# Output weights loaded seven chunks ahead, and background sums pinned in issue order and marked on both halves

## The chip, the cores and the metric

The kernel runs on one core of one Trainium2 chip. The metric is the device time of one execution in microseconds (us). The engines are TensorE (PE in the profile, with PEld for its weight loads), VectorE (DVE), ScalarE (ACT), GpSimd (POOL) and SyncE (SP), which here only issues DMAs. Sixteen DMA engines move the data: q1 is the queue that SP's transfers use, q0 the one that GpSimd's use.

## The reference

One decoder layer on 512 tokens of width 2048, in float32. The input is normalised and multiplied by one wide matrix; its columns are split into the latents of an MLA branch (8 heads, decoupled rotary key), the queries, keys and values of a forgetting-attention branch ("fox", 8 heads), and a gate for each. Both branches run causal softmax attention, are gated, joined and multiplied by `w_out`; the result is normalised and added to the input.

```python
h = _rms_norm(x, g_pre)
proj = h @ w_in
(q_lat, kv_lat, k_rope_raw, gate_mla, fq, fk, fv, f_logit, gate_fox) = jnp.split(proj, split_points, axis=-1)
o_mla = _mla_branch(q_lat, kv_lat, k_rope_raw, ...) * jax.nn.silu(gate_mla)
o_fox = _fox_branch(fq, fk, fv, f_logit, b_forget) * jax.nn.silu(gate_fox)
o = jnp.concatenate([o_mla, o_fox], axis=-1) @ w_out
return x + _rms_norm(o, g_post)
```

## The kernel before

**Precision.** A float32 operand is used as a sum of two reduced-precision parts, hi and lo. A product is three matmuls, hi by hi, hi by lo and lo by hi (`mm3`, lines 150 to 152).

**Weights.** They come in chunks of up to 128 x 1024, numbered in the order of use in one list (220 chunks). `load` issues the DMA of chunk i into a tile raw (lines 242 and 259 issue it on SP). `divide` makes whi by a cast on ACT (line 279) and wlo by a subtraction on DVE (line 282). `chunk(i, ahead_load=4, ahead=2)` is called where chunk i is needed: it loads up to chunk i + ahead_load and divides up to i + ahead. The whi and wlo tiles are three deep. Where a raw tile lies is decided in `raw_tile` (line 224): six buffers of a pool of its own in the stage of the latents and MLA gates (`deep`), a slot, a pool of three buffers called wp, or, late in the output stage, every other three chunks a second pool of three (`more`). Slots are 28 places of 4 KB a partition (line 88) that hold most other tiles: normalised input, head operands, gates, fetched operands, partial results.

**Fewer products.** The blocked products (values v, latents l, MLA gates m, the values of the MLA branch u, and the output, o) are done with seven half-size products in place of eight, named p1, p2, p4, q6, g7, g5 and g3. Some need sums of weight blocks, t7, t6, t5 and t4. Sums of activations are made on DVE, and most are put away in HBM by GpSimd (`away_steps`, line 944; its stores are line 953, tiles awaymg and awayog) and fetched again by SP (line 987).

**Sums of weights.** Some are made when the chunk is used: the second block is loaded beside the first (line 250) and joined on DVE (line 269); joins are asked for up to two chunks before the division. The rest are made in the background, in HBM, by DMAs alone. The list `bg` holds, in order, the tiles of v, l, m, u and o. `add_step(n)` (line 314) does three things: GpSimd accumulates the second block into tile n-1 (line 320), SP copies the first block into tile n (line 324), and SP copies 16 numbers of the weight tile just used into tile n+1 (line 326), a mark: the next step's copy writes the same bytes, so it has to wait for the mark, and the mark for that weight tile. So a step is tied to the progress of the products. For u a block is a strided view with four dimensions and is moved in two halves of 512 columns (`alike`, line 306); the mark lies in the first.

**When steps come.** `paced` (line 561) counts finished pieces of products and calls `add_step` when the pace is reached; tiles of o are twice as wide and count double. The pace is 20, 8, 12 and 4.9 in turn, 1000 (none) from line 1429 to line 1505, and 4.5 after it.

**Order.** A scheduler arranges each engine's instructions at compile time from its own estimate of when each is ready; the order of the source gives the priority. `in_order` (line 132) pins an instruction behind what was traced before it on its engine; the joins are pinned so, and the casts while `deep` is set.

**Stages in time.** First projection, to about 42 us; values and fox gates, to about 230; fox heads, to about 425; the products of latents and MLA gates, to about 580; MLA heads, to about 730; then the output products (lines 1755 to 1825), which hold 56 chunks. `three` (line 1789) issues six of the fourteen output products. Each product takes its chunks by the loop in `product` (line 1030).

Of the kernel before, what the change touches and what calls it, by code (L numbers as in the profile page):

```python
# [16 lines left out]
ALU = mybir.AluOpType  # L17
# [49 lines left out]
def tile_hybrid_layer(  # L67
# [16 lines left out]
    nc = tc.nc  # L84
    pe, act, dve, pool = nc.tensor, nc.scalar, nc.vector, nc.gpsimd
# [14 lines left out]
    def slot(name, dt=F32, shape=(P, 2, S)):  # L100

        return sp.tile(list(shape), dt, tag="s", name=name)
# [29 lines left out]
    def in_order(*instructions):  # L132

        for i in instructions:
            tc.keep_in_program_order(i)
# [13 lines left out]
    def mm3(o, ah, al, bh, bl, first, last, **kw):  # L149
        pe.matmul(o, ah, bh, start=first, stop=False, **kw)  # L150
        pe.matmul(o, ah, bl, start=False, stop=False, **kw)  # L151
        pe.matmul(o, al, bh, start=False, stop=last, **kw)  # L152
# [55 lines left out]
    def add_chunks(w, cols, nk, per, width, first_k=0, single=0):  # L208


        first = len(chunks)
        k = 0
        while k < nk:
            n = min(1 if k < single else per, nk - k)
            chunks.append((w, cols, first_k + k, n, width))
            k += n
        return range(first, len(chunks))

    raws, ready, up_chunks, early = {}, {}, set(), set()
# [4 lines left out]
    def raw_tile(i):  # L224
        if deep and deep[1] <= i < deep[2] and (i - deep[1]) % (DEEP + 3) < DEEP:
            return deep[0].tile([P, 1024], F32, tag="raw", name=f"raw{i}", bufs=DEEP)
        if i in up_chunks:
            return slot(f"raw{i}", shape=(P, 1024))
        if i <= prods["g7", "v"][-1] and i % 5 < 2:
            return vr.tile([P, 1024], F32, tag="raw", name=f"raw{i}", bufs=2)  # L230
        pool = more[0] if more and (i - more[1]) % 6 < 3 else wp
        return pool.tile([P, 1024], F32, tag="raw", name=f"raw{i}", bufs=3)

    def load(i, small=None):

        w, cols, k, n, width = chunks[i]
        assert state["step"] >= needs.get(i, -3) + 2
        if cols is None:

            raw = raw_tile(i)  # L240
            for a, b in alike(raw, w):
                nc.sync.dma_start(a, b)
            raws[i] = raw
            if k is not None:
                if seconds and i not in early:
                    pool, bufs = seconds
                    second = pool.tile([P, 2, 512], F32, tag="second", name=f"second{i}", bufs=bufs)
                else:
                    second = slot(f"second{i}")
                nc.sync.dma_start(second, k)  # L250
                raws[i] = raw, second.rearrange("p k c -> p (k c)")
            return
        if i < 2:
            raw = slot(f"raw{i}", shape=(P, 1024))
        else:
            raw = raw_tile(i)
        v = raw[:, : n * width].rearrange("p (k c) -> p k c", k=n)
        for at, off, cnt in cols:
            (nc.sync if cnt >= P or small is None else small).dma_start(
                v[:, :, at : at + cnt],  # L260
                w[0, k * P : (k + n) * P, off : off + cnt].rearrange("(k p) c -> p k c", p=P),
            )
        raws[i] = raw

    def join(i):

        if isinstance(raws.get(i), tuple):
            raw, second = raws[i]
            tc.keep_in_program_order(dve.tensor_tensor(out=raw, in0=raw, in1=second, op=ALU.add))  # L269
            raws[i] = raw  # L270
# [16 lines left out]
    def prepare(i):  # L287
        while state["divided"] < min(len(chunks), i + 1):
            divide(state["divided"])
            state["divided"] += 1  # L290

    def chunk(i, ahead_load=4, ahead=2):
        upto = i + ahead_load
        if deep:
            upto = max(upto, min(i + DEEP + 2, deep[2] - 1, state["loaded"] + i % 2))
        while state["loaded"] < min(len(chunks), upto + 1):
            load(state["loaded"])
            state["loaded"] += 1
        prepare(i + ahead)
        for k in range(i + ahead + 1, min(state["loaded"], i + ahead + (3 if deep else 2))):  # L300
            join(k)
        return ready.pop(i)

    W, made = {}, {}
    bg = []

    def alike(to, w):

        if len(w.shape) == 4:
            to = to.rearrange("p (k h x) -> p k h x", k=2, h=4)  # L310
            return [(to[:, k], w[:, k]) for k in range(2)]
        return [(to if len(w.shape) == 2 else to.rearrange("p (k c) -> p k c", k=2), w)]

    def add_step(n, mark):


        if n > 0:
            to, _, second = bg[n - 1]
            for a, b in alike(to, second):
                pool.dma_start(a, b, accum_op=ALU.add)  # L320
        if 0 <= n < len(bg):
            to, first, _ = bg[n]
            for a, b in alike(to, first):
                nc.sync.dma_start(a, b)
        if n + 1 < len(bg):
            nc.sync.dma_start(bg[n + 1][0][0:1, 0:16], mark)

    def sum_blocks(g, block, late, width=512, nj=4):

# [14 lines left out]
    prods = {}  # L344
# [43 lines left out]
    first = add_chunks(w_in, [(0, O_KR - L4, KL), (KL, O_F, NH)], NK, 2, KL + NH, single=2)  # L388
# [157 lines left out]
    def pump(n=1):  # L546
        for _ in range(n):
            if todo:
                todo.popleft()()
# [11 lines left out]
    def paced(w):  # L561

        if state["step"] <= len(bg):
            state["tiles"] += 1
            wide = 0 <= state["step"] < len(bg) and bg[state["step"]][0].shape[1] > 1024
            pace = state["pace"] * (1 + wide)
            if state["tiles"] >= pace:
                state["tiles"] -= pace
                add_step(state["step"], w[0:1, 0, 0:16].bitcast(F32))
                state["step"] += 1  # L570
# [367 lines left out]
    def head_steps(j, names, raw_of, place):  # L938

        return operand_steps("o", j, (o_of[K1[j]], o_of[K2[j]]), names, raw_of, place)  # L940
# [53 lines left out]
    def divisions(n, of):  # L994
        return [lambda j=j: part_fetched(n, of, j) for j in range(2 if of == "o" else 4)]
# [13 lines left out]
    def product(name, g, parts, o, first, last, rate=1, at=None, held=0, side=(), turned=False):  # L1009


        side = deque(side)
        kk = 0

        def step(j, kk, t, hi, lo):
            if not turned:
                mm3(
                    o[t], *parts(kk, t), hi[:, j, :], lo[:, j, :], first and kk == 0, last and kk == 7,
                    skip_group_check=True,
                )  # L1020
                return
            for f in range(2):
                c = slice((2 * t + f) * P, (2 * t + f + 1) * P)
                mm3(
                    o[t][:, f * HALF : (f + 1) * HALF], hi[:, j, c], lo[:, j, c], *parts(kk),
                    first and kk == 0 and f == 0, last and kk == 7, skip_group_check=True,
                )

        rng = list(prods[name, g])
        for i in rng[: len(rng) - held]:  # L1030
            hi, lo = chunk(i)
            for j in range(2):
                if at is not None and kk == at[0]:
                    at[1]()
                for t in range(2):
                    step(j, kk, t, hi, lo)
                kk += 1
                pump(rate)
                paced(hi)
                if side and not held and kk % 2 == 0:  # L1040
                    side.popleft()()
        w = [chunk(i, ahead=0) for i in rng[len(rng) - held :]]
        if w:
            side.popleft()()
        for t in range(2):
            for m in range(2 * len(w)):
                step(m % 2, kk + m, t, *w[m // 2])
            if w:
                finish(t, 2, o[t])
# [172 lines left out]
    todo.extend([*fs[13:], *rot[:3]])  # L1222
    A = two_of(proj_bank, "va")
    product("p1", "v", x_block(0, 0), A, True, True)
    drain()
    pa, pb = v_block("vpa"), v_block("vpb")
# [306 lines left out]
    def halves(a):  # L1533
        return [a[:, t, :] for t in range(2)]
# [55 lines left out]
    for p in range(4):  # L1590
        if p == 3:
            first = divisions("a11", "o") + [s for j in (2, 3) for s in head_steps(j, ("a11",), tmp, part_slot)]
# [3 lines left out]
        if p == 0:  # L1596
# [3 lines left out]
            p1 = slot("up1")  # L1600
            for t in range(2):
                act.copy(p1[:, t, :], A[t])
            p1 = halves(p1)
# [150 lines left out]
    p1 = [slot(f"p1{g}") for g in range(2)]  # L1754
# [6 lines left out]
    p1 = [halves(a) for a in p1]  # L1761
# [99 lines left out]
```

## Time and profile before

| | us |
|---|---|
| median of 3 runs | 895.2 (894.72 to 896.06) |
| the profiled execution | 896.48 |
| its span, first to last instruction | 894.7 |
| mean granted TensorE clock | 0.995 |
| moved by DMA | 225.07 MB, mean 252 GB/s |

The profile is of one execution. A line of the timeline is start, duration, engine (a q behind it: its sequencer), source line, operation, what it writes and reads (buffer numbers left out), count, and in brackets the idle time before it and what ended that. In the list of waits a line is who waited, for whom, the total, how often and the longest. A line of the chain of waits is start, duration and what the chain ran through.

### The profile page before, as it was taken

To read this page: it belongs to the slowest core of one execution; us is meant where nothing else is said; L and a number is where in the kernel's file an instruction comes from. 1 tells how busy PE (TensorE), PEld (TensorE's weight loads), DVE (VectorE), ACT (ScalarE), POOL (GpSimd) and SP (SyncE) were. 2 spreads that over 40 slices of the span, in tenths; PEclk is the share of its full clock that TensorE was granted. 3 is DMA by queue.
4 is the path that set the end of the run, shared out by engine and by line. 5 is a ranking of instruction groups with operands and counts; after the bars stand their busy time and mean duration, and the time that the engine had idled before them with its cause. 6 is when DMAs were issued, how large, how long until landed. Compare 5 with 4: busy or idle time off the path is not lost.

```text
span 894.7 us, 12701 instructions
## 1 busy us (share of the span) xinstructions
PE 882.5 (99%) x4486; PEld 748.8 (84%) x4486; DVE 660.3 (74%) x1106; ACT 462.5 (52%) x841; POOL 72.9 (8%) x92
## 2 busy tenths in 40 slices
PE   9999999999999999999999999999999999999996
PEld 9988887888888888888998999787888888888885
DVE  4679995548656636476588898978787895988785
ACT  7944443334344424345545565546465776646383
POOL 0111110001111211010000000000000000000021
PEclk9999999999999999999999999999999999999998
DMA  9998798889899998897899884799878537799878
GB/s 304 298 269 237 204 358 275 247 224 316 260 280 271 249 229 210 234 254 178 270 411 407 322 294 141 152 278 201 209 166 215 151 113 236 226 326 320 265 211 249
DMA packets 139235, 225.07 MB, mean 252 GB/s; under 512 B 16898, under 2 KB 68892, under 8 KB 138148
## 3 DMA queue, kind: packets, MB, share of 16 engines
q1 hardware_dynamic: 124660, 184.19, 63.3%
q0 software_dynamic: 13776, 39.85, 21.8%
q8 instruction: 35, 0.57, 0.2%
q10 hardware_dynamic: 736, 0.22, 0.1%
q14 instruction: 28, 0.23, 0.1%
HBM read 209.53 MB, written 69.22 MB: 312 GB/s over the span
## 4 chain that ended last, share of the span: by engine, by line
PE 87%; DMA 6%; DVE 3%; ACT 2%; issue 1%; SPq 0%; POOL 0%; ACTq 0%; DVEq 0%; POOLq 0%
PE fq L150 3%; PE fk L150 3%; PE fk L152 3%; PE fk L151 3%; PE fq L152 3%; PE fq L151 3%; PE in L614 3%; PE sm L657 3%; PE fg L150 2%; PE fg L151 2%; PE fg L152 2%; PE oa L150 2%; PE oa L152 2%; PE oa L151 2%; PE sf L657 2%; DMA raw<-t4u 1%
## 5 line engine op out<-in xcount | busy, mean ns | idle before, releaser
L282 DVE TENSOR_TENSOR wlo<-raw,whi 128x1024 fp32r<-128x1024 f32 (+3 forms) x220 | 260.7, 1188 | 135.7 <-ACT whi L279 128.8
L279 ACT CAST whi<-raw 128x1024 fp32r<-128x1024 f32 (+3 forms) x220 | 224.3, 1023 | 233.5 <-PE fk L151 35.3
L150 PE MATMUL fk<-h,whi 128*128 128x512 f32 x128 | 52.5, 410 | 0.0
L150 PE MATMUL fq<-h,whi 128*128 128x512 f32 x128 | 50.8, 397 | 0.0
L150 PE MATMUL fg<-h,whi 128*128 128x512 f32 x128 | 50.3, 393 | 0.0
L152 PE MATMUL fk<-h,wlo 128*128 128x512 f32 x128 | 50.2, 392 | 0.0
L151 PE MATMUL fk<-h,whi 128*128 128x512 f32 x128 | 50.1, 392 | 0.0
L152 PE MATMUL fq<-h,wlo 128*128 128x512 f32 x128 | 50.0, 390 | 0.0
L151 PE MATMUL fq<-h,whi 128*128 128x512 f32 x128 | 49.9, 390 | 0.0
L152 PE MATMUL fg<-h,wlo 128*128 128x512 f32 x128 | 49.9, 390 | 0.0
L151 PE MATMUL fg<-h,whi 128*128 128x512 f32 x128 | 49.8, 389 | 0.0
L675 ACT ACTIVATE pf<-pf,stf 128x128 f32<-128x128 f32 (+3 forms) x32 | 18.0, 562 | 61.1 <-DVE stf L666 61.1
L269 DVE TENSOR_TENSOR raw<-raw,second 128x1024 f32<-128x1024 f32 x32 | 39.0, 1218 | 0.4 <-DMA second<-in_w_out_dram 0.4
L614 PE MATMUL in<-whi,h 128*128 128x328 f32 x128 | 30.0, 321 | 0.0
L150 PE MATMUL mq<-ln,whi 128*128 128x512 f32 x72 | 29.2, 406 | 0.0
L152 PEld LDWEIGHTS fk<-h,wlo 128*128 128x128 f32 x128 | 24.0, 188 | 5.5
L152 PEld LDWEIGHTS fq<-h,wlo 128*128 128x128 f32 x128 | 24.0, 188 | 5.3
L152 PEld LDWEIGHTS fg<-h,wlo 128*128 128x128 f32 x128 | 24.0, 188 | 5.1
L151 PE MATMUL mq<-ln,whi 128*128 128x512 f32 x72 | 28.2, 392 | 0.0
L152 PE MATMUL mq<-ln,wlo 128*128 128x512 f32 x72 | 28.2, 392 | 0.0
L151 PEld LDWEIGHTS fg<-h,whi 128*128 128x128 f32 x128 | 24.1, 188 | 4.7
L150 PEld LDWEIGHTS fg<-h,whi 128*128 128x128 f32 x128 | 24.0, 188 | 4.7
(610 smaller groups left out, 2418.9 us busy)
## 6 DMA issues: line engine op xcount, KB each, us to landing
raw<-in_w_in_dram SPq DMA_DIRECT2D x96, 512.0 KB
raw<-in_w_out_dram SPq DMA_DIRECT2D x32, 512.0 KB
second<-in_w_in_dram SPq DMA_DIRECT2D x24, 512.0 KB
bmg<-awaymg SPq DMA_DIRECT2D x20, 256.0 KB
awaymg<-rmg POOLq DMA_DIRECT2D x8, 512.0 KB, 7.7
raw<-t6v SPq DMA_DIRECT2D x8, 512.0 KB
t7o<-in_w_out_dram SPq DMA_DIRECT2D x4, 1024.0 KB
t7o<-in_w_out_dram POOLq DMA_DIRECT2D x4, 1024.0 KB, 11.7
```

The costliest lines, as they stand in the source:

```text
L150: pe.matmul(o, ah, bh, start=first, stop=False, **kw)
L151: pe.matmul(o, ah, bl, start=False, stop=False, **kw)
L152: pe.matmul(o, al, bh, start=False, stop=last, **kw)
L269: tc.keep_in_program_order(dve.tensor_tensor(out=raw, in0=raw, in1=second, op=ALU.add))
L279: cast = act.copy(hi[:, :m], raw[:, :m])
L282: dve.tensor_tensor(out=lo[:, :m], in0=raw[:, :m], in1=hi[:, :m].bitcast(F32), op=ALU.subtract)
L614: pe.matmul(banks[t][:, :n], a[k][:, tss[t]], b[:, j, :], start=k == 0 and m == 0, stop=k == NK - 1 and m == 2,)
L657: pe.matmul(s[:, :nn], a[:, qs], c[:, :nn], start=(i == 0), stop=(i == len(pairs) - 1))
L675: act.activation(p, p, AF.Exp, bias=st[:, 0:1], scale=unit, accum_out=st[:, 1:2])
```

## The change

Three edits, in `raw_tile`, `add_step` and `product`.

- In the output products a chunk's call loads up to seven chunks ahead; elsewhere four, as before. From the first output chunk on, each chunk whose number is a multiple of three has its raw tile in a slot.
- GpSimd's accumulation of a background sum is pinned behind what was traced before it on GpSimd.
- Where a background tile is moved in two halves (u, four tiles), each half gets a mark.

```diff
     def raw_tile(i):
         if deep and deep[1] <= i < deep[2] and (i - deep[1]) % (DEEP + 3) < DEEP:
             return deep[0].tile([P, 1024], F32, tag="raw", name=f"raw{i}", bufs=DEEP)
-        if i in up_chunks:
+        if i in up_chunks or i >= prods["p1", 0][0] and i % 3 == 0:
             return slot(f"raw{i}", shape=(P, 1024))
...
         if n > 0:
             to, _, second = bg[n - 1]
             for a, b in alike(to, second):
-                pool.dma_start(a, b, accum_op=ALU.add)
+                in_order(pool.dma_start(a, b, accum_op=ALU.add))
         if 0 <= n < len(bg):
             to, first, _ = bg[n]
             for a, b in alike(to, first):
                 nc.sync.dma_start(a, b)
         if n + 1 < len(bg):
-            nc.sync.dma_start(bg[n + 1][0][0:1, 0:16], mark)
+            to, first, _ = bg[n + 1]
+            nc.sync.dma_start(to[0:1, 0:16], mark)
+            if len(first.shape) == 4:
+                nc.sync.dma_start(to[0:1, 512:528], mark)
...
         for i in rng[: len(rng) - held]:
-            hi, lo = chunk(i)
+            hi, lo = chunk(i, 7 if g in (0, 1) else 4)
```

## The prediction

> **What bounds the kernel now.** I read the page first, then the list of TensorE's waits.
>
> ```profile
> span 894.7 us, 12701 instructions
> ...
> PE 882.5 (99%) x4486; PEld 748.8 (84%) x4486; DVE 660.3 (74%) x1106; ACT 462.5 (52%) x841; POOL 72.9 (8%) x92
> ```
> ```profile
> PE mix L1706 <- ACT scaler L1705: 2.2, 1, 2.2
> PE sm L657 <- ACT mw L127: 1.1, 1, 1.1
> PE warm L169 <- DVE warm L164: 1.1, 1, 1.1
> PE vg L151 <- DVE wlo L282: 0.7, 1, 0.7
> PE gcm L151 <- DVE wlo L282: 0.6, 1, 0.6
> PE uC L150 <- DVE mk L140: 0.5, 1, 0.5
> PE od L151 <- DVE wlo L282: 0.3, 1, 0.3
> ```
>
> TensorE is busy in 882.5 of 894.7 us, so an edit gains only what it takes out of the few waits, and costs whatever new wait it makes. In the list a row is who waited, for whom, us in total, times, longest. The waits that better fed weights could shorten are those for wlo: 0.7, 0.6 and 0.3, together 1.6 us. Only the last, at tile od, lies in the output stage, where the deeper loading acts. The others (mix, sm, warm, uC) end on arithmetic of ACT and DVE that no edit touches.
>
> So the three edits are searched for new waits. Two touch queues outside the output stage, and the one that looks like bookkeeping, the pinning of GpSimd's accumulating DMAs, moves the most. I went on to the timeline of POOL's instructions.
>
> ```profile
> 189.88 1.17 POOL L320 DMA_DIRECT2D t7l<-in_w_in_dram  x1 [3.02 <-DMA t7l<-in_w_in_dram]
> 210.55 1.50 POOL L1194 DMA_DIRECT2D v_away<-vc  x2 [19.50 <-DVE vc L1152]
> ...
> 394.65 0.81 POOL L320 DMA_DIRECT2D t4o<-t6o  x1 [11.88 <-DMA t6o<-t7o]
> ...
> 406.03 1.16 POOL L320 DMA_DIRECT2D t7o<-in_w_out_dram  x1 [9.80 <-DMA t7o<-in_w_out_dram]
> ...
> 459.89 0.53 POOL L953 DMA_DIRECT2D awayog<-rog  x1 [1.81 <-DVE rog L963]
> 567.29 0.88 POOL L320 DMA_DIRECT2D t6o<-t7o  x1 [106.86 <-DMA t6o<-in_w_out_dram]
> ```
> ```profile
> 558.49 0.26 SPq L326 DMA_DIRECT2D t6o<-whi  x1
> ```
>
> These rows run out of the source's order. One background step issues, in this order, the accumulation of tile n-1 (line 320), the first load of tile n (324) and the mark of tile n+1 (326). The mark of the second t6o came at 558.49, because the pace is 1000 between lines 1429 and 1505. The same step accumulates the first t4o, and that ran at 394.65; the next step's accumulation, of the second t7o, ran at 406.03. The scheduler hoisted both by some 160 us, ahead of the awayog stores, which the source issues from line 1444 on, inside the products of lines 1452 and 1458.
>
> **The change part by part.** *Pinning line 320.* A pinned instruction comes after everything traced before it on its engine. So the two accumulations can start no earlier than the last awayog store, at 459.89 + 0.53 = 460.4 us. Their data are there, as both ran by 406, and nothing else is on POOL until 567, so I expect them at once, one behind the other. What do they meet? The next rows are DMA queues in a stretch (packets, MB, share of the 16 engines) and two stretches (length, busy us of PE, PEld, DVE, ACT and POOL, clock, DMA share, GB/s).
>
> ```profile
> q0 software_dynamic: 497, 2.36, 46.4%
> ```
> ```profile
> 444.00:492.00 48.00, 48.00 (x312) 44.04 (x311) 37.22 (x38) 25.11 (x30) 1.07 (x2) 1.00 1.04 410
> 492.00:520.00 28.00, 28.00 (x193) 26.10 (x192) 25.00 (x29) 14.67 (x18) 0.00 (x0) 1.00 0.81 285
> ```
>
> The first row is the stretch 394 to 420, in which GpSimd's queue q0 did these two and a 0.26 MB store. It held the engines for 46.4% of 26 us = 12.06 us; by bytes the two are 2.10 of 2.36 MB, 10.7 us. From 444 to 492 the engines are full (share 1.04, 410 GB/s) with the latent and gate weights. Putting 10.7 to 12.06 us of work there delays the loads behind it by that over 1.04, which is 10.3 to 11.6 us; I take 10.9. Slack returns only from 492 on (share 0.81).
>
> How much lead have those loads? Each of the four chunks of the product at line 1469 (p4 of the gates, tile gbm) needs a raw load and a second one, joined on DVE at line 269. I follow the last of them.
>
> ```profile
> 468.14 0.40 PE L150 MATMUL gm<-whi,h 128*128 128x512 f32 x1
> ...
> 479.05 0.39 PE L150 MATMUL gbm<-whi,h 128*128 128x512 f32 x1
> ```
> ```profile
> 421.30 6.48 SPq L259 DMA_DIRECT2D raw<-in_w_in_dram  x3
> ...
> 471.69 0.38 SPq L250 DMA_DIRECT2D second<-in_w_in_dram  x1
> ```
> ```profile
> q1 hardware_dynamic: 7272, 16.36, 76.0%
> ```
> ```profile
> 479.06 1.22 DVE L269 TENSOR_TENSOR raw<-raw,second 128x1024 f32<-128x1024 f32 x1
> 480.20 0.69 DVE L140 TENSOR_TENSOR bmq<-bmq 128x512 fp32r<-128x512 f32 x1
> 480.91 1.23 DVE L282 TENSOR_TENSOR wlo<-raw,whi 128x1024 fp32r<-128x1024 f32 x1
> ```
>
> Four chunks take 479.05 - 468.14 = 10.91 us, 2.73 each. The second load was issued at 471.69; the SP queue's requests from 421.30 up to it (28 of 0.524 MB, 4 of 0.262) make 15.7 MB, and q1 had moved 16.36 MB from 418 to 477, so it landed near 476. Its join starts at 479.06, a spare of about 3.0 us (at least 0, at most the 7.4 us since its issue). Behind that join, on DVE in order, stands the wlo of gbm's third chunk, done at 480.91 + 1.23 = 482.14 and wanted by that chunk's second matmul, at 479.05 + 2 x 2.73 + 0.2 = 484.7: another 2.5 us. So a late landing is hidden up to 5.5 us (2.5 to 9.9). With 10.9 late, TensorE waits 5.4 us; the bounds are 10.3 - 9.9 = 0.4 and 11.6 - 2.5 = 9.1. I take 5.4, nearest to the counted landing. Behind the waiting join stand all later DVE splits of this stage, and behind those TensorE; nothing downstream gives it back, since TensorE has 48.00 of 48.00 and 28.00 of 28.00 us to do.
>
> A long wait may also slow the clock. Stretch 612 to 616, right after the sm and uC waits:
>
> ```profile
> 612.00:616.00 4.00, 4.00 (x15) 3.43 (x14) 2.94 (x9) 1.48 (x6) 0.00 (x0) 0.57 0.57 144
> ```
>
> The clock was 0.57 over 4 us after waits of 1.1 + 0.5 us: about 1.7 us lost. Here the slow stretch would begin after the first late chunk, while the next loads are still catching up, so it mostly runs inside the 5.4 us; it goes into the upper bound only. The Trainium skill (TensorE: Matmul & The Clock Gate, Part 1) drops the clock only after an idle window of about 3.4 us; by that rule the 1.6 us here would not have been enough, and a loss split into pieces under 3.4 us would cost nothing more. The trace disagrees, and I go by it.
>
> The same pin moves other accumulations behind stores, such as the t7l of 189.88 behind the v_away of 210.55. These are half the size, and the engines are not full around them, so I count 0, with half a microsecond either way.
>
> *Marks on both halves.* The second halves of the four u tiles had no mark.
>
> ```profile
> L324 SPq DMA_DIRECT2D t7u<-in_w_ukv_dram x2: 557/614/670, 19.6 to 322.2; - x2
> ```
>
> One half was loaded at 19.6 us, the other at 322.2. The change moves four issues of about 0.6 us on SP, and two accumulations on POOL, from the first projection to the 320s, and adds four marks. Queued behind them on SP are the forgetting heads' weight loads (line 259). Neither place shows a TensorE wait in the list above, so this costs 0; without that cover it would be 4 x 0.6 = 2.4 us of SP.
>
> *Output weights seven ahead, every third in a slot.* Stretch 714 to 884 holds the output products:
>
> ```profile
> 714.00:884.00 170.00, 169.62 (x781) 139.96 (x780) 137.79 (x210) 101.86 (x168) 7.13 (x8) 1.00 0.76 243
> ```
>
> TensorE is idle there for 0.38 us in 170. That bounds the gain at about 0.4, or 0.9 with slow restarts after two waits (one 0.50 us matmul in the last row below); I take 0.5. The chain of waits leads the od wait back to a weight load of 9.10 us amid the fetches of operand sums:
>
> ```profile
> 786.52 5.93 DMA bog<-awayog
> 792.53 9.10 DMA raw<-t7o
> ...
> 806.42 0.50 PE od L151
> ```
>
> A DMA share of 0.76 leaves room to load earlier. The price is up to three of 28 slots, which the fetched sums want too.
>
> **Sum.** +5.4 - 0.5 = +4.9 us. The profiled execution took 896.48 us (span 894.7 plus 1.8 around it), 1.3 over the median of 895.2. On its own time that gives 901.4, and 900.1 as a median.
>
> **The rivals.** *Hidden clump.* The two accumulations fit into the loads' lead: if the fourth join's data have the full 9.9 us, or the queue serves the loads first, the wait is 0.4 or nothing and the output gain remains: 894.7, no change. For it: the joins run without a wait now, and the landing is counted, not seen. Against it: engines without a gap from 444 to 492 must push something back.
>
> *The wlo waits are load waits.* The clump is hidden, and the three waits for wlo (vg, gcm, od) end on weight loads, not on DVE's own order. The change takes transfers out of the stretches in front of the first two and loads the third earlier, so all three go: 0.7 + 0.6 + 0.3 and 0.27 for each restart (a matmul of 0.50 where 10.91 / 48 = 0.23 is the step) is 2.4, which gives 892.8, faster. It decides once each of these loads lands some 0.7 us sooner. For it: the od wait does follow a load. Against it: the other two stand on DVE, which takes splits in order.
>
> *Slots run out.* The raw tiles hold slots that the fetched bog parts need. A bog fetch takes 5.93 us and a split follows it; if it starts a chunk (2.73) or two late, up to 4 us come on top. With the clump hidden that is 899; it decides once more than 25 of the 28 slots are taken when the sums are fetched.
>
> *The depth does not arrive.* Two thirds of the chunks still share buffers three deep, so loads asked for seven ahead may wait for the same releases; then the output stage is unchanged, and the time is 900.6 with the clump or 895.2 without.
>
> **How the numbers follow.** Clump felt, 900.1: 0.58. Hidden clump, 894.7: 0.18. Load waits, 892.8: 0.11. Slots alone, 899: 0.08. No depth and no clump, 895.2: 0.05. A measurement of this kernel tells about 0.2%, 1.8 us, from no change. Clump felt is slower by more than that except at its low end (0.02), so slower is 0.56 + 0.08 = 0.64, same 0.18 + 0.05 + 0.02 = 0.25, faster 0.11. The range leaves out the load waits below and reaches to the hidden clump, with the spread of the runs, 893.9; above it goes to 895.2 + 9.1 - 0.5 = 903.8, leaving under 0.1 out with the slow clock on top. Clump felt alone spans 895.1 to 903.8 by its bounds.
>
> **What would show it.** In POOL's timeline t4o and t7o follow the last awayog directly, near 460. In 394 to 420 the DMA share falls; in 466 to 480 q0 takes most of the engines. TensorE shows waits for wlo between 476 and 490, up to 5 us in sum, perhaps a clock below 1.00, and everything later is shifted by that. The od wait is gone. The t7u loads stand together in the 320s. I am wrong if TensorE stays full from 470 to 490, if t4o and t7o stand elsewhere, or if new waits appear in the output stage.

## The result and the profile after

The kernel after takes 907.89 us (median of 4 runs, 906.1 to 909.0) against 895.33 before (4 runs): a ratio of 1.0137 (95% interval 1.0119 to 1.0156), 12.6 us slower. The forecast was slower by 4.9 with an upper end of 903.8, so the direction held and the size did not. The profiled execution took 907.93 us, 11.45 more than that of before; its span is 11.3 longer.

The page of the kernel after, then its list of TensorE's waits (who waited, for whom, total, times, longest):

```profile
span 906.0 us, 12697 instructions
...
PE 885.3 (98%) x4486; PEld 751.2 (83%) x4486; DVE 659.7 (73%) x1106; ACT 461.7 (51%) x841; POOL 72.8 (8%) x92
```
```profile
PE pvf L150 <- ACT fv3h L139: 4.7, 1, 4.7
PE gbm L151 <- DVE wlo L282: 2.3, 1, 2.3
...
PE gm L151 <- DVE wlo L282: 1.9, 1, 1.9
...
PE sm L660 <- ACT mw L127: 0.4, 1, 0.4
PE od L151 <- DVE wlo L282: 0.4, 1, 0.4
```

Three waits are new: gbm and gm, which the forecast named, and pvf, which it did not. Two stretches show what they cost beside their own length (the columns are those of the stretches in the prediction; the granted clock stands third from the end):

```profile
265.00:270.00 5.00, 4.80 (x13) 3.78 (x14) 1.65 (x4) 2.42 (x7) 2.00 (x2) 0.54 0.91 294
491.00:496.00 5.00, 4.33 (x13) 3.46 (x13) 4.52 (x5) 2.77 (x5) 0.00 (x0) 0.66 1.04 412
```

The first lies right behind the wait for pvf, the second behind that for gbm. TensorE was busy for 4.80 and 4.33 us of them; at a clock of 0.54 and 0.66, 2.2 and 1.5 us of that are lost.

The account: 4.7 + 2.3 + 1.9 of waits and 2.2 + 1.5 of clock make 12.6 us. At the first matmul of tile uC (in the MLA heads), behind both places, the kernel after is 14.0 us late (622.13 for 608.14). Of that, 0.8 is there already at the first matmul of the first projection (6.61 for 5.78), and 0.6 is not assigned to rows. The span is only 11.3 us longer, because the next stretch was slower in the profiled execution of before: sm waited 1.1 us (0.4 after), a slow stretch followed (0.57 over 4 us), and from the first uC to the next uA it took 9.6 us, against 7.2 after:

```profile
608.14 0.39 PE L150 MATMUL uC<-whi,suq 128*128 128x512 f32 x1
...
617.70 0.40 PE L150 MATMUL uA<-whi,ln 128*128 128x512 f32 x1
```
```profile
622.13 0.39 PE L150 MATMUL uC<-whi,suq 128*128 128x512 f32 x1
...
629.36 0.40 PE L150 MATMUL uA<-whi,ln 128*128 128x512 f32 x1
```

**The place that was forecast.** POOL's timeline:

```profile
467.58 0.53 POOL L956 DMA_DIRECT2D awayog<-rog  x1 [1.81 <-DVE rog L966]
468.10 0.92 POOL L320 DMA_DIRECT2D t4o<-t6o  x1
468.66 1.56 POOL L320 DMA_DIRECT2D t7o<-in_w_out_dram  x1
```

The two accumulations follow the last awayog directly, as argued; everything there is 7.7 us later than before, 6.9 of it from the first place. The queues from 472 to 484 (packets, MB, share of the 16 engines):

```profile
q0 software_dynamic: 429, 2.15, 79.5%
q1 hardware_dynamic: 429, 1.07, 24.6%
```

Both queues had work, and both sent 429 packets; by thirds of the stretch it is 175 to 170, 107 to 113 and 147 to 146. But one of q0 held an engine for 12 us x 16 x 0.795 / 429 = 0.356 us, one of q1 for 0.110. So the weight loads got a quarter of the engines. Twelve us of before, at the same place in the program (464 to 476), show q1 with 4.43 MB and 93.2%, for 1.07 and 24.6% here. The Trainium skill (DMA: Bandwidth & Descriptors, Queues, rings and completion order) says that an engine takes turns between its queues packet by packet; the equal counts agree, and since the turns are not of equal length, q1's share falls far below a half. On DVE the joins then wait for their second operand, the first for 5.04 us:

```profile
483.25 1.22 DVE L269 TENSOR_TENSOR raw<-raw,second 128x1024 f32<-128x1024 f32 x1 [5.04 <-DMA second<-in_w_in_dram]
```

**The place that was not.** The same pin moved accumulations of l. POOL's timeline after, which answers to the row of 189.88 before:

```profile
211.01 1.49 POOL L1197 DMA_DIRECT2D v_away<-vc  x2 [31.40 <-DVE vc L1155]
212.48 0.94 POOL L320 DMA_DIRECT2D t6l<-t7l  x1
213.07 1.57 POOL L320 DMA_DIRECT2D t7l<-in_w_in_dram  x1
231.71 2.89 POOL L1197 DMA_DIRECT2D v_away<-vo  x4 [17.07 <-DVE vo L1155]
234.59 0.94 POOL L320 DMA_DIRECT2D t6l<-t7l  x1
235.17 1.58 POOL L320 DMA_DIRECT2D t7l<-in_w_in_dram  x1
```

Two pairs now run directly behind stores. Three stretches of before, which the prediction does not show, and then the same of after:

```profile
186.00:212.00 26.00, 26.00 (x117) 21.52 (x116) 17.76 (x20) 9.53 (x14) 3.46 (x4) 1.00 0.86 249
212.00:232.00 20.00, 19.89 (x88) 16.16 (x87) 16.26 (x20) 10.31 (x12) 1.61 (x3) 1.00 0.90 281
232.00:246.00 14.00, 14.00 (x67) 11.67 (x66) 8.49 (x27) 4.50 (x10) 3.40 (x5) 1.00 0.98 286
```
```profile
186.00:212.00 26.00, 26.00 (x117) 21.53 (x116) 17.31 (x19) 9.99 (x14) 0.99 (x2) 1.00 0.64 205
212.00:232.00 20.00, 19.60 (x87) 15.87 (x86) 15.63 (x19) 10.31 (x12) 2.93 (x4) 1.00 0.93 262
232.00:246.00 14.00, 14.00 (x66) 11.71 (x65) 6.61 (x22) 2.76 (x8) 4.75 (x6) 1.00 1.01 288
```

The DMA share fell from 0.86 to 0.64 where there was room, and the work went to where the engines were at 0.90 and 0.98 already. How that reaches TensorE is told by the chain of waits of the kernel after (start, length, what):

```profile
235.64 14.36 DMA t7l<-whi
...
250.67 0.57 SPq L324
...
252.40 12.32 DMA fv<-v_away
...
265.20 0.79 PE pvf L150
```

The first row is a mark, 64 bytes. It took 14.36 us to land; before, the load that waits for it was issued 9.1 us behind it (234.85 to 243.94). SP's next background load waits for it, and behind that load, in SP's order, stands the fetch of the values fv. In SP's timeline of before the same three stand earlier:

```profile
234.85 0.57 SPq L326 DMA_DIRECT2D t7l<-whi  x1
...
243.94 0.56 SPq L324 DMA_DIRECT2D t7l<-in_w_in_dram  x1
...
246.32 0.39 SPq L1165 DMA_DIRECT2D fv<-v_away  x1
```

So fv was issued 6.1 us later, at 252.40 for 246.32. Its transfer was no slower: 12.3 us after, and at most 12.4 before, where ACT casts it from 258.68. Before, it landed in time; now TensorE waits 4.7.

### The profile page after: what moved, and what is told of

Its sections match the earlier page's. It is cut to its first block, busy times and chain, and to the rows that moved or that the text cites. A ratio compares the mean times of both kernels' runs of the same rounds, so it can differ in the third digit from the quotient of the medians.

```text
span 906.0 us, 12697 instructions
## 1 busy us (share of the span) xinstructions
PE 885.3 (98%) x4486; PEld 751.2 (83%) x4486; DVE 659.7 (73%) x1106; ACT 461.7 (51%) x841; POOL 72.8 (8%) x92
## 4 chain that ended last, share of the span: by engine, by line
PE 81%; DMA 8%; DVE 6%; ACT 2%; issue 1%; SPq 0%; POOL 0%; DVEq 0%; ACTq 0%; POOLq 0%
PE in L617 3%; PE fk L150 3%; PE fk L152 3%; PE fk L151 3%; DMA second<-in_w_in_dram 3%; PE sm L660 3%; PE fq L150 2%; PE fg L150 2%; PE fg L151 2%; PE fg L152 2%; PE fq L152 2%; PE fq L151 2%; DVE wlo L282 2%; PE mq L152 2%; PE mq L150 2%; PE mq L151 2%
## 5 line engine op out<-in xcount | busy, mean ns | idle before, releaser
L150 PEld LDWEIGHTS fk<-h,whi 128*128 128x128 f32 x128 | 24.4, 191 | 4.5
L151 PEld LDWEIGHTS fg<-h,whi 128*128 128x128 f32 x128 | 24.1, 188 | 4.7
```

## The experiments

The theory: the pin alone costs the time, at two places, both because GpSimd's transfers were moved to where the DMA engines are full. The first rival: the marks or the output stage's edit share in it. Every time stands beside that of the kernel before, measured with it.

**The parts alone.** e1_pin has only the in_order on line 320; e2_no_pin has the rest of the change; e3_marks only the marks; e4_output only the edits of `raw_tile` and `product`.

> The pin alone. Theory: the pin makes both new waits, at pvf near 260 (4.7 us and 2.0 of slow clock) and at gm and gbm near 484 to 495 (4.2 and 2.0), less 1.9 given back at sm near 609. So 906 to 909 us, both waits in the list. Rival: the wait at pvf comes from the marks or the slots; then 899 to 902, and only gm and gbm wait.

> All but the pin: marks on both halves, seven ahead, slots. Theory: 895.3, within 0.8, no wait at pvf, gm or gbm; od unchanged at 0.3 to 0.4. Rival: 899 to 902, with the wait at pvf.

> Only the marks on both halves of u. Both theories: 895.3 within 0.5, unless the four issues of the second halves, now near 320, delay a weight load of the forgetting heads; then a wait there of up to 2.4.

> Only the output stage: seven ahead and slots. If the wait at od follows a load: 894.8, the wait of 0.3 gone. If it follows the order of DVE's work: 895.3, od waits 0.3 to 0.4 as before.

| | us | before | ratio (95%) |
|---|---|---|---|
| e1_pin | 907.53 | 894.61 | 1.0135 (1.011 to 1.016) |
| e2_no_pin | 895.51 | 894.61 | 1.0013 (1.0005 to 1.0022) |
| e3_marks | 895.64 | 894.61 | 1.0009 (0.9999 to 1.0019) |
| e4_output | 894.53 | 894.61 | 1.0000 (0.9992 to 1.0008) |

The pin alone gives the whole loss; the rival falls. Without it, 0.13% is left (e2, at most 0.22), of which the marks may be 0.09; the output stage's edit costs and gains nothing that can be told. The waits of e1_pin:

```profile
PE gbm L151 <- DVE wlo L282: 2.8, 1, 2.8
PE sf L657 <- DVE stf L666: 2.6, 1, 2.6
PE pvf L150 <- ACT fv3h L139: 2.3, 1, 2.3
```

Both places show again. In the first, part of the wait now stands at sf: there a fetch of nk (14.58 us in the chain of waits) came late as well as that of fv, so the wait shows at one or the other.

In e4_output the tiles t7o were asked for from 780.79 on (790.63 before), so the depth arrived. The wait at od stayed at 0.4. DVE's timeline of e4_output, in front of it:

```profile
799.51 1.22 DVE L269 TENSOR_TENSOR raw<-raw,second 128x1024 f32<-128x1024 f32 x1
801.92 1.23 DVE L282 TENSOR_TENSOR wlo<-raw,whi 128x1024 fp32r<-128x1024 f32 x1 [1.19 <-ACT whi L279]
803.07 1.22 DVE L269 TENSOR_TENSOR raw<-raw,second 128x1024 f32<-128x1024 f32 x1
...
805.54 1.23 DVE L282 TENSOR_TENSOR wlo<-raw,whi 128x1024 fp32r<-128x1024 f32 x1 [0.65 <-ACT whi L279]
```

Join on DVE, cast on ACT, subtraction on DVE, then the next join: a cycle of 3.6 us (801.92 to 805.54), while TensorE takes 2.73 for a chunk. Each chunk loses 0.9 of its lead, until TensorE waits. No load stands in this cycle: none of the joins waits for one.

**The two places apart.** Line 320 pinned for some accumulations only:

```diff
+            moved = n - 1 in [made[k] for k in KEYS]
             for a, b in alike(to, second):
-                pool.dma_start(a, b, accum_op=ALU.add)
+                go = pool.dma_start(a, b, accum_op=ALU.add)
+                if moved:
+                    in_order(go)
```

```diff
+    last = lat_block(1, 0)[1][:, 0, 0:16]
+    in_order(pool.tensor_tensor(out=late, in0=last, in1=last, op=ALU.add))
     set_pace(4.5)
```

In e5_pin_l KEYS are the first two t6l and the second and third t7l; in e6_pin_o the first t4o and the second t7o. e7_pin_o_half halves the transfers of e6 (`x[..., : x.shape[-1] // 2]` for a and b; the other half of these sums is left out). e8_pin_o_late is e6 with the second diff: a pinned GpSimd instruction that reads the last sums of the latents, so that the two follow it.

> The kernel before, with only the four accumulations of l pinned that ran ahead of the v_away stores. Theory: this is the first of two places. Waits between 240 and 272 of 4.7 to 7 us in sum (the pin alone showed 5.5 there) with 2 to 3.5 of slow clock, no wait at gm or gbm, up to 1.9 given back at sm: 900 to 905. Rival: the accumulations of v that the pin moves too are needed for that wait; then 895 to 896.

> Only the accumulations of the first t4o and the second t7o pinned. Theory: the second place alone. gm and gbm wait 4.1 to 4.2 in sum, 2.0 of slow clock, up to 1.9 back at sm: 899.5 to 901.5, no wait at pvf over 1. Rival: they hurt only because the loads are late already after the first place; then under 897.

> As the run before, but each of the two accumulates only half its columns (the other half of these two sums is left out). Theory, bytes: 5.5 us less of engine time, so the 4.2 of waits fall to under 0.5 and the clock stays: 894.5 to 896.5. Rival, the order or the issue: as with all the bytes, 899.5 to 901.5.

> The same two pinned, and moved on to about 547 by a small GpSimd instruction ahead of them that reads the last sums of the latents; from 552 to 567 the share of the DMA engines was 0.34 in the kernel before. Theory: gm and gbm don't wait, and the freed stretch near 400 lets loads run ahead: 893.5 to 895.5. Rival, being pinned behind the stores costs by itself: over 898.

| | us | before | ratio (95%) |
|---|---|---|---|
| e5_pin_l | 900.44 | 894.89 | 1.0059 (1.0038 to 1.0079) |
| e6_pin_o | 901.92 | 894.89 | 1.0070 (1.0047 to 1.0093) |
| e7_pin_o_half | 897.51 | 894.89 | 1.0020 (1.0004 to 1.0035) |
| e8_pin_o_late | 894.92 | 894.89 | 0.9998 (0.9983 to 1.0013) |

The places add up: 5.5 + 7.0 = 12.5 us, against 12.9 for the pin alone and 12.6 for the change. e5_pin_l shows the wait for pvf alone, at 4.0, a little under the 4.7 that was expected. e6_pin_o, just over the 901.5 that was expected, shows one wait of 3.8 at gm, and behind it a long stretch at half the clock:

```profile
480.00:487.00 7.00, 6.19 (x15) 4.89 (x16) 5.31 (x6) 3.88 (x7) 0.00 (x0) 0.52 1.02 401
```

TensorE was busy for 6.19 of the 7 us, so 6.19 x 0.48 = 3.0 us went to the slow clock; with the wait that is 6.8 us. How much of the 3.0 is a cost of its own is taken up below. Half the bytes (e7) leave 0.3 of waits for wlo at gbm and 2.6 of the 7.0 us; that is a little over what was expected, and more than those waits explain. Moved to 552 (e8, below), the same two transfers cost nothing, though they are pinned: the place costs, not the pin.

```profile
551.68 0.89 POOL L321 DMA_DIRECT2D t4o<-t6o  x1 [0.28 <-issue]
```

The freed stretch near 400 gave no gain.

**How the first place works.** One number changes in e9_pin_l_fv (from e5_pin_l) and e10_fv (from the kernel before):

```diff
-            todo.insert(12, lambda vt=vt: load_v(3, vt))
+            todo.insert(9, lambda vt=vt: load_v(3, vt))
```

SP then issues the fetch of fv ahead of the two background loads that wait for marks. e11_pin_l_half halves the transfers of e5 and leaves out the other half. e12_change_mended is the whole change with the fetch ahead and e8's instruction.

> The four accumulations of l pinned, and the first fetch of fv issued on SP ahead of two background loads that wait for their marks instead of behind them. Theory, SP's order: the accumulations make the mark land late, and fv stands behind the load that waits for it; fetched ahead, pvf waits under 1 us: 895 to 897. Rival, the engines' time: fv itself is slow wherever it stands; pvf still waits over 2.5, 898.5 to 902.

> The kernel before with fv fetched ahead in the same way. pvf waited between 0 and 2.6 us in the profiles of kernels without the pin of l, so fv lands at the brink. If that costs the median something: 893.5 to 894.7. If not, or if it is paid back in a shorter wait at sm: 894.9 within 0.5.

> The four accumulations of l pinned, each over half its columns (the other half of these four sums is left out). Theory, bytes: the mark lands sooner and pvf waits under 1.5: 895 to 897. Rival, the order of issue on GpSimd: 899 to 902 as with all the bytes.

> The whole change, with both remedies: the accumulations of the first t4o and the second t7o moved on to about 547, and fv fetched ahead. Theory, two places and nothing else: no wait over 1 at pvf, gm or gbm, 894 to 897. Rival, a third cost (the pinned accumulations of v, the marks, the slots): over 898.

| | us | before | ratio (95%) |
|---|---|---|---|
| e9_pin_l_fv | 894.81 | 895.22 | 1.0002 (0.9986 to 1.0017) |
| e10_fv | 894.39 | 895.22 | 0.9984 (0.9972 to 0.9995) |
| e11_pin_l_half | 894.48 | 895.22 | 0.9990 (0.9979 to 1.0000) |
| e12_change_mended | 898.06 | 895.22 | 1.0041 (1.0018 to 1.0064) |

In e9_pin_l_fv the fetch goes out ahead, and the load behind it waits as long as ever:

```profile
242.94 0.44 SPq L1168 DMA_DIRECT2D fv<-v_away  x1
249.13 0.56 SPq L327 DMA_DIRECT2D t7l<-in_w_in_dram  x1
```

The wait at pvf is gone, and the 5.5 us with it. So both links of the chain are shown. Fewer bytes end the wait (e11): the load that waits for the mark is issued at 241.99 and fv at 244.86, against 249.03 and 251.41 in e5. Taking fv out from behind the mark ends it too (e9). e10_fv came out 0.16% under the kernel before (0.05 to 0.28). A reason would be that fv lands at the brink there, too (the wait at pvf was 0.9 in the profile of e3, 0.5 in e4's, 2.6 in e8's); but e16_fv_late below has the same fetch ahead and shows no gain, so the gain is not confirmed.

e12 was expected at 894 to 897 and came to 898.06, its runs between 895.0 and 905.3. Four more kernels looked for a third cost: e13_pin_v and e18_pin_u pin only the accumulations of v and of u; e14_pin_mended is e12 without the marks and the output stage's edit, e15_mended_but_v is e12 with v not pinned, e17_pin_lo_mended pins only l and o, with both remedies. e16_fv_late joins the remedies without the pin on l, as the candidate for a faster version.

> The kernel before, with only the accumulations of v pinned; two of them move behind the stores of awaymg at 85 and 112. If these are the third cost: 897 to 898.5, with a wait near 139 or at vp that varies from run to run. If not: 895 within 0.6.

> The pin alone with both remedies, without the marks and the output stage's edit. If the third cost lies in the pin (v): 897 to 899. If it lies in the marks or the output stage together with the moved transfers: 894 to 895.7.

> The whole change with both remedies and the accumulations of v not pinned. If v is the third cost: 894 to 895.7. If not: 897 to 899, as with v.

> The kernel before with fv fetched ahead and the two accumulations of o at about 547: the candidate for a version that beats both kernels. 893.7 to 894.7; the wait at sm stays under 0.5, since the stretch before 420 is freed for loads. If fv ahead alone is all the gain: as that run, a ratio of 0.998 to 0.999.

> The accumulations of l and of o pinned, with both remedies; those of v and u as in the kernel before. If the remaining 2 us come from l and o together (fv ahead mends the one wait, other waits of the first place come and go): 896 to 898, with runs over 899. If they come from the moved accumulations of u: 894.3 to 895.5, no run over 899.

> The kernel before with only the accumulations of u pinned; the two second halves move from 27 to near 329. If they are the remaining cost: 896 to 898. If not: 895 within 0.6.

| | us | before | ratio (95%) |
|---|---|---|---|
| e13_pin_v | 895.17 | 894.47 | 0.9999 (0.9983 to 1.0015) |
| e14_pin_mended | 896.56 | 894.47 | 1.0037 (1.0010 to 1.0064) |
| e15_mended_but_v | 896.72 | 894.47 | 1.0028 (1.0009 to 1.0046) |
| e16_fv_late | 895.41 | 894.47 | 1.0008 (0.9996 to 1.0019) |
| e17_pin_lo_mended | 896.93 | 894.76 | 1.0032 (1.0011 to 1.0053) |
| e18_pin_u | 894.28 | 894.76 | 0.9996 (0.9984 to 1.0007) |

Neither v nor u costs anything that can be told, and neither the marks nor the output stage's edit is needed: what stays, some 2 us, comes with l and o together (e17), though each with its remedy costs nothing (e9, e8). e14 and e15 fell between the two values that were expected of them. e16 missed: 893.7 to 894.7 was expected, it took 895.41, and at up to 0.19% over the kernel before the two remedies together may hold part of those 2 us. It comes in some runs only (three of e17's twelve took 901.5 to 904.1, the others 894.9 to 897.2), and the profiled one, at 895.87, shows no wait that explains it. The fetch of nk, which waited in e1_pin and is not moved, may be it; that wasn't tried, and the cause stays open.

## Why the prediction was wrong

**The step that failed** is the sentence "These are half the size, and the engines are not full around them, so I count 0, with half a microsecond either way." The tiles are half the size, but four accumulations move, so together they carry as many bytes as the two of o (4 x 0.524 MB). And "not full around them" holds for the place that they left (a share of 0.86 from 186 to 212), not for the places where the pin puts them (0.90 and 0.98). The term was 5.5 us (e5_pin_l) instead of 0, and outside its bounds: a mark landed late there, and the fetch of fv stood behind it on SP. The prediction asked what the accumulations of o meet where they are put, and did not ask it of those of l.

**The forecast place was right in mechanism, low in size.** t4o and t7o followed the last awayog, q0 took most of the engines, the joins waited for their second load, and TensorE waited for wlo: 4.2 us in the change and 3.8 in e6_pin_o, where 5.4 was forecast within 0.4 to 9.1. The wait showed one product earlier too, at gm. The whole place costs 7.0 (e6_pin_o), inside the bounds of 0.4 to 9.1.

That the slow stretch "mostly runs inside the 5.4 us" is borne out by e6_pin_o. DVE and TensorE there, behind the wait at gm:

```profile
482.45 1.23 DVE L269 TENSOR_TENSOR raw<-raw,second 128x1024 f32<-128x1024 f32 x1 [1.69 <-DMA second<-in_w_in_dram]
...
484.20 1.22 DVE L282 TENSOR_TENSOR wlo<-raw,whi 128x1024 fp32r<-128x1024 f32 x1
...
490.50 1.22 DVE L282 TENSOR_TENSOR wlo<-raw,whi 128x1024 fp32r<-128x1024 f32 x1
```
```profile
486.10 0.63 PE L151 MATMUL gbm<-wlo,h 128*128 128x512 f32 x1
...
492.10 0.39 PE L151 MATMUL gbm<-wlo,h 128*128 128x512 f32 x1
```

TensorE went on at 480.81, but a join still waited for its load until 482.45, and the wlo of gbm's first chunk was done only at 485.42. At full rate, 12 matmuls of 0.23 us on from 480.81, TensorE would have wanted it at 483.5 and waited again. The third chunk's wlo was done at 491.72 and used at 492.10. So by these rows, an estimate, a full clock would have won about 0.4 us there, not 3.0 (in the change about 1.0, where that wlo was done at 497.94 and used at 498.96): the loads set the pace. The term that was too small is the lateness of the loads, some 6.6 us in e6_pin_o (7.0 less 0.4) for 5.4. The first place is different: with the same four accumulations and fv ahead (e9_pin_l_fv) TensorE runs on without a delay there, so what it loses in the slow stretch behind pvf is a cost of its own.

**That "nothing downstream gives it back"** stands. The profiled execution of the kernel after does come 2.3 us nearer to that of before behind uC, but this is no effect of coming late: from the first uC to the next uA, e13_pin_v, which reaches uC 0.2 us ahead of before, takes 6.8 us, and all kernels but before (9.6) and e2_no_pin (9.5) take 6.5 to 8.0. The profiled execution of before was slow there, and its time lies 1.3 us above the median. The 1.9 us at sm in the expectations for e1, e5 and e6 fall with this.

**The output stage** was read from a chain that happened to pass a load. The wait at od is set by the cycle of join, cast and subtraction; the 0.5 of gain was 0 (e4_output). The rival of the three load waits falls by the same rows: gcm is 0.8 and vg 0.5 in the change, od 0.4. The rival that the depth does not arrive falls too; it arrived and hid nothing. Slots did not run out: no new wait shows in the output stage. The marks on both halves cost nothing that can be told (e3_marks), as forecast. The hidden clump falls with the waits at gm and gbm.

The whole, then: +5.4 - 0.5 was summed; the runs give +7.0, +5.5 and 0.

## What to carry to other kernels

An edit that pins one kind of instruction moves every instruction of that kind; each one that moves is a term of the sum, and the stretch it moves into must be read, not assumed. A tiny transfer that others wait for can take long where the engines are busy (a mark of 64 bytes took 9 to 14 us here), so put urgent fetches ahead of such waits on the issuing queue, not behind them. Where TensorE stops for some 4 us, count a slow stretch behind the stop, but ask what TensorE would have waited for next: where that is still late, the slow stretch costs little of its own. And before a difference of two profiles is called an effect, see whether kernels that lack its cause show it, too.

## What the runs showed of the hardware

Two full queues took turns by packets: 429 to 429 from 472 to 484, with accumulating packets of 0.356 us (5.0 KB) beside loads of 0.110 (2.5 KB).

The clock after a wait did not follow its length alone. In the change the wait of 1.9 us at gm was followed by matmuls at full rate, and in e8_pin_o_late so was one of 2.6 at pvf (first row); in e1_pin one of 2.6 at sf was followed by a stretch at 0.57 (second row):

```profile
262.00:267.00 5.00, 4.13 (x19) 3.37 (x20) 2.56 (x5) 3.02 (x7) 2.01 (x2) 1.00 1.07 282
```
```profile
245.00:249.00 4.00, 3.37 (x8) 2.69 (x9) 1.49 (x9) 1.43 (x3) 0.00 (x0) 0.57 1.03 199
```

All three waits of 3.8 to 4.7 us (pvf in the change and e5_pin_l, gm in e6_pin_o) were followed by a slow stretch. Behind the wait of 2.3 at pvf in e1_pin matmuls ran at full rate for 1.8 us, from 267.54, and only then at half. And the time at half the clock (matmuls 0.43 us apart for 0.23) comes in one length or its double. From the mean granted clock of wider stretches, waits included, it is 0.12 x 14 / 0.5 = 3.4 us in the change (486 to 500, granted 0.88), 3.4 in e1_pin (242 to 252, 0.83), 6.8 in the change (258 to 275, 0.80) and 6.9 in e6_pin_o (476 to 491, 0.77).

The Trainium skill (TensorE: Matmul & The Clock Gate, Part 1) has the activity counted in free-running windows of about 3.4 us; that two equal waits differ agrees with windows that do not start with the wait, and so do the lengths of 3.4 and 6.8; that 2.6 us sufficed once does not agree with a full idle window as the condition.
